# When half-finished weight sums are issued in a gated recurrence, and where its gate products stand: one change to a fused two-layer decoder kernel

## The chip, the cores and the metric

The kernel runs on one core of a Trainium2 chip. TensorE (PE) multiplies, VectorE (DVE) and ScalarE (ACT) do elementwise work, GpSimd (POOL) does small elementwise work and issues one queue of DMAs, SyncE (SP) issues the other queue. The metric is the device time of one execution in microseconds (us). The kernel before takes 2057.65 us, the median of three runs (2055.35, 2057.65, 2061.02).

## The reference, cut to what matters

Two layers on 1024 tokens of width 1024, all in float32. Layer 0 mixes tokens with a gated linear recurrence (HGRN2), layer 1 with a convolution module. Each mixer is followed by a residual layer norm, a squared-ReLU MLP of width 4096, and another residual layer norm.

```
proj = h @ w_in;  q, fz, v, g = split(proj, 4)              # layer 0
q = silu(q);  f = lb + (1 - lb) * sigmoid(fz);  k = 1 - f
S_t = diag(f_t) S_{t-1} + k_t v_t^T;   o_t = S_t^T q_t       # 8 heads of 128
o = o * rsqrt(mean(o^2) + 1e-6) * norm_g                     # a norm for each head
mix = (o * silu(g)) @ w_out                                  # the gate product
x = layer_norm(alpha * x + mix)
ff = square(relu(x @ ffn_w1[i])) @ ffn_w2[i]                 # up, then down
x = layer_norm(alpha * x + ff)
```

## The kernel before, in words

**Products.** A float32 product is made of three fp32r matmuls with a high and a low part of each operand (hi·hi, hi·lo, lo·hi). Most large products go by a fast 2x2 scheme: seven products of half-size blocks, of which several are of sums of blocks. Each of these seven is called a form; a raw weight block or a sum of blocks is cast to its high part by ACT, and DVE subtracts to get the low part. A form of the projections or of the up product is 12 or 24 matmuls of 128x512.

**Weight sums in DRAM.** The down product (`ffn_w2`) of each layer needs four sums of blocks for each of its eight slices of the inner width (chunks). They are made ahead, in DRAM, by DMAs that add on arrival. One set belongs to one chunk and has four sums. It starts with two plain copies of 1 MB (`L419`, `L420`), goes on with one adding DMA of 1 MB (`L421`), and then with two adding DMAs of 0.5 MB (`L423` twice), where each of these three needs the landing of what went before. Adding DMAs are issued from POOL. There are 16 sets, for two layers of eight chunks; the list `to_sum` gives their order. `block_sums` issues 12 of them in the recurrence stage, all from POOL. `sum_pieces` makes two more in the first MLP, after its chunks 0 and 2: seven pieces, one behind each form that follows, where the four copies (0.5 MB each, `L435`) go out from SP behind a tiny DMA that waits for the form (`L434`), and the three adds from POOL (`L440`). The last two sets are made later, in layer 1.

**The recurrence stage.** After the value projection, a loop runs over 12 pairs of column blocks (`PAIRS`: a pair makes the query and forget columns of one head, or the gate columns of two heads), 7 forms each. A form is cut into four slots of three matmuls, and each slot calls `slot()`, which is a tick. Python lists order everything: `later(n, job)` puts a job n ticks on, `step()` lets one or two heads' generators (`recurrence(h)`) go on by one of 18 steps, and two heads overlap, nine steps apart. So each engine's instruction order is written out by hand here; what waits at run time is decided by semaphores.

The steps that matter here: step 13 transposes the keys; step 14 makes the outer products for the state of four chunks of 128 tokens (`outer`), and one tick later DVE makes the chain of states (`chain`: a copy, then one instruction for each chunk); step 15 makes the outputs (`attend`), and one tick later comes the second chain and `settle(0)`; step 16 makes the other outputs, and one tick later comes `settle(1)`. A `settle` is the norm of half of the tokens for one head: ACT squares with a sum (`L755`), POOL a `tensor_scalar` (`L756`) and a power (`L538`), and four ticks later ACT scales the outputs (`L761`). Then PE transposes them (`give`), ACT takes them out (`L774`), and SP stores them in DRAM.

**The gate product.** `gate_turn`, called at every tick, loads a stored half-head (`u`) back, and when the gate for it is ready and nine ticks have gone by since that load, DVE multiplies them (`t<-u,t`, 128x512) and SP stores the result (`zd`). The last two heads do this in the seam, a list of jobs that runs beside the last pair and loads the output projection's weights.

**Order of the sums before.** In the pair loop, every sixth form starts a set: the first copy at once, the second 6 ticks on, the adds 12, 24 and 36 ticks on. POOL's order, with the norms between, follows from these ticks.

**The first MLP.** Up product: eight chunks of seven forms (the first two chunks have two of theirs made earlier). Weights are loaded and turned into forms three ahead (`fw.ahead(3)`). Beside this, `spare` turns weights of layer 1 into high and low parts and stores them (`ready`): DVE copies one column, POOL copies it on (`L1464`, `L1472`) so that the next load waits for it, ACT casts (`L1465`). From here on the order is not by hand: a scheduler with its own model of time sets it.

Of the kernel before, what the change touches and what calls it, by code (L numbers as in the profile page):

```python
# [8 lines left out]
F32 = mybir.dt.float32  # L9
# [3 lines left out]
ALU = mybir.AluOpType  # L13
PSUM = bass.MemoryType.PSUM

P = 128
# [3 lines left out]
H = 8  # L20
# [248 lines left out]
def body(ctx, tc, d, out):  # L269
    nc = tc.nc  # L270
# [128 lines left out]
    def block_sums(name, layer, c, after=None, gap=0, adds=None):  # L399
# [24 lines left out]
        for i, part in enumerate(parts):  # L424
            later((i + 1) * gap, part)

    def sum_pieces(name, layer, c):

        t = sums[name, layer, c] = dram.tile([4, P, 1024], F32, name=f"sum_{name}{layer}{c}")
        v, w = t.rearrange("a p n -> p a n"), d[name][layer, c].rearrange("a p n -> p a n")  # L430

        def copy(i, q):
            def go(after):
                nc.sync.dma_start(out=t[i : i + 1, 0, 0:1], in_=after)  # L434
                nc.sync.dma_start(out=v[:, i], in_=w[:, q])  # L435

            return go

        def add(out, x, **kw):
            return lambda after: nc.gpsimd.dma_start(out=out, in_=x, accum_op=ALU.add, **kw)  # L440

        def chained(i):
            return add(v[:, i], v[:, i - 1], max_dma_last_dim=4096)

        return [copy(0, 0), copy(1, 2), add(v[:, 0:2], w[:, 2:4]), copy(2, 0), chained(2), copy(3, 1), chained(3)]
# [208 lines left out]
    def recurrence(h):  # L654
# [159 lines left out]
        later(1, lambda: (chain(range(NTB, nk)), settle(0)))  # L814
        yield
        attend(range(NTB, 2 * NTB))
        later(1, lambda: settle(1))
        if h < H - 2:
            for half in range(2):
                load_values(2 * h + 2 + half)  # L820
# [110 lines left out]
    def gate_turn():  # L931
        now = ticks[0]
        if to_load and len(loaded) < 2 and done.get(to_load[0], now) <= now - 7:
# [1 line left out]
            u = p1("u")  # L935
            nc.sync.dma_start(out=u, in_=od[at[0]][at[1]])
            loaded.append((at, u, now))
        if loaded and loaded[0][0] in gates and loaded[0][2] <= now - 9:
            (h, half), u, _ = loaded.pop(0)
            g = gates.pop((h, half))  # L940
            mul(g, u, g)

            def store():
                nc.sync.dma_start(out=zd[half][:, h, :], in_=g)
                stored[h, half] = ticks[0]

            later(2, store)
# [79 lines left out]
    for p, (kind, j) in enumerate(PAIRS):  # L1027
# [7 lines left out]
        for i in ORDER:  # L1035
# [3 lines left out]
                    step()  # L1039
            pair_product(p, i, made.pop(0), st)  # L1040
            later(2, make_form)
            if (7 * p + ORDER.index(i)) % 6 == 1 and len(to_sum) > 4:
                block_sums(*to_sum.pop(0), gap=12)
        if kind == "q":
            later(4, lambda j=j: recs.append(j))
    early_out = ((0, 0), (1, 0), (2, 0))
# [9 lines left out]
    tick(100)  # L1056
    assert not waiting and not loaded and not to_load and not gates, (waiting, gates)
    order.close()
    oT = [o[0] for o in oT]


# [429 lines left out]
    for c in range(NFC):  # L1491
        for i in ORDER[2 if c < 2 else 0 :]:
# [4 lines left out]
            up.form(c, i, f)  # L1497
            if summing:
                summing.pop(0)(f[:1, 1, :1].bitcast(F32))
        if c in (0, 2):  # L1500
            summing += sum_pieces(*to_sum.pop(0))
        if c == 0:
            up.settle(1)
# [479 lines left out]
```

## Time and profile before

| what | value |
|---|---|
| median of three runs | 2057.65 us (2055.35 to 2061.02) |
| the profiled execution's own time | 2057.38 us |
| span of its trace | 2055.6 us |
| PE busy | 2024.2 us (98%) |
| mean granted TensorE clock | 0.998 |
| recurrence and seam in the trace | about 84 to 424 us |
| first MLP, chunks 1 to 7 | about 553 to 810 us |

How to read it: PE is busy nearly all the time, so the time can fall only where PE waits or where its clock is lower. An instruction's row in the timeline gives its start, its length, and in brackets the idle time of its engine just before, with what ended it. A row of the waits gives the total, the number of waits and the longest. A row of the windows gives the busy time of each engine in a stretch, the granted clock (1.00 is full) and the share of the 16 DMA engines that was busy; that share counts overlapping packets and reaches 1.08.

### The profile page before, as it was taken

The numbers are of one execution on the slowest core, as the hardware profiler recorded it, in microseconds if no ns is written. First come the engines' busy times: TensorE is split into PE (matmuls) and PEld (weight loads), VectorE is DVE, ScalarE is ACT, GpSimd is POOL, SyncE is SP. The second block draws the span as 40 slices with busy tenths as digits, with TensorE's granted clock in tenths as the row PEclk, the third lists the DMA queues.
The fourth block names the chain that finished last, engine by engine and source line by source line (L and its number), as shares of the span: only waits on it lengthen the run. The fifth ranks groups of instructions, "written<-read, shape, count | busy, mean of one in ns | idle before, by whom it ended". The sixth has DMA issues, their size and how long they took to land. (4 is left out here: it accounts for less than half of the span.)

```text
span 2055.6 us, 29682 instructions
## 1 busy us (share of the span) xinstructions
PE 2024.2 (98%) x11144; PEld 1669.3 (81%) x11144; DVE 1488.7 (72%) x1978; ACT 1092.3 (53%) x1725; POOL 394.7 (19%) x405
## 2 busy tenths in 40 slices
PE   8999999999999999999999999999999999999998
PEld 7888887888788888888888888888888888888886
DVE  8698887877866665666557898889589666754456
ACT  5456565631654655444443776488615555443343
POOL 0112232111000000000001799079210000100002
PEclk9999999999999999999999999999999999999999
DMA  4788999942399786999998755487659778995542
GB/s 187 216 206 229 263 244 250 268 185 89 125 324 298 275 302 215 374 341 325 336 339 294 303 185 187 191 329 268 255 210 344 247 236 299 392 293 195 194 154 103
DMA packets 183120, 517.55 MB, mean 252 GB/s; under 512 B 17984, under 2 KB 49856, under 8 KB 181824
## 3 DMA queue, kind: packets, MB, share of 16 engines
q1 hardware_dynamic: 167488, 456.93, 61.7%
q0 software_dynamic: 15488, 58.72, 12.3%
q8 instruction: 87, 1.43, 0.3%
q14 instruction: 57, 0.47, 0.1%
HBM read 380.85 MB, written 201.85 MB: 283 GB/s over the span
## 5 line engine op out<-in xcount | busy, mean ns | idle before, releaser
L204 PE MATMUL ps<-dw,dh 128*128 128x512 f32 x2688 | 611.6, 389 | 0.9 <-ACT dh L72 0.7
L204 PEld LDWEIGHTS ps<-dw,dh 128*128 128x128 f32 x2688 | 504.1, 188 | 106.3 <-ACT dh L72 1.1
L204 PE MATMUL ps<-x1f,fw 128*128 128x512 f32 x1344 | 307.8, 390 | 4.3 <-ACT fw L72 2.9
L204 PEld LDWEIGHTS ps<-x1f,fw 128*128 128x128 f32 x1344 | 251.4, 188 | 59.2 <-issue 2.7
L204 PE MATMUL ps<-xf,fs 128*128 128x512 f32 x1008 | 250.0, 399 | 3.5 <-issue 1.9
L204 POOL TENSOR_TENSOR cb<-cb,prod 128x512 f32<-128x512 f32 x168 | 222.5, 1333 | 14.4 <-ACT prod L1614 4.1
L204 PEld LDWEIGHTS ps<-xf,fs 128*128 128x128 f32 x1008 | 184.8, 189 | 42.8 <-issue 2.1
L204 DVE TENSOR_TENSOR dh<-dh 128x1024 fp32r<-128x1024 f32 x112 | 136.3, 1222 | 109.6 <-ACT dh L72 106.5
L204 DVE SCALAR_TENSOR_TENSOR ps<-u,par,ps 128x512 f32<-128x512 f32 x296 | 205.9, 749 | 10.7 <-ACT ps L1626 9.3
L204 PE MATMUL ps<-xa,wa 128*128 128x512 f32 x864 | 203.6, 393 | 1.3 <-DVE xa L204 0.9
L72 ACT CAST dh<-dh 128x1024 fp32r<-128x1024 f32 x112 | 117.2, 1050 | 146.3 <-DMA dh<-hf 141.2
L204 DVE TENSOR_TENSOR dw<-dr,dw 128x1024 fp32r<-128x1024 f32 x112 | 136.2, 1222 | 76.2 <-ACT dw L72 75.5
L204 PEld LDWEIGHTS ps<-xa,wa 128*128 128x128 f32 x864 | 160.2, 188 | 35.1 <-DVE xa L204 1.3
L72 ACT CAST dw<-dr 128x1024 fp32r<-128x1024 f32 x112 | 117.1, 1052 | 134.7 <-PE ps L204 114.0
L1614 ACT ACTIVATE prod<-u,par 128x512 f32<-128x512 f32 x168 | 119.2, 725 | 35.4 <-POOL cb L204 34.8
L538 POOL TENSOR_TENSOR mv<-mv,nhalf 128x1 f32<-128x1 f32 x32 | 42.2, 1319 | 403.9 <-DVE mv L204 393.6
L204 PE MATMUL ps<-w,oT 128*128 128x512 f32 x384 | 89.9, 392 | 1.3 <-ACT oT L952 0.8
L204 PE MATMUL ps<-xb,wa 128*128 128x512 f32 x384 | 91.1, 393 | 0.0
L204 PE MATMUL ps<-vw,xf 128*128 128x512 f32 x336 | 79.4, 398 | 6.1 <-ACT vw L455 5.5
L204 PEld LDWEIGHTS ps<-w,oT 128*128 128x128 f32 x384 | 71.4, 188 | 16.6 <-ACT oT L952 1.2
L204 PEld LDWEIGHTS ps<-xb,wa 128*128 128x128 f32 x384 | 71.1, 188 | 14.4
L1465 ACT CAST spare<-next 128x1024 fp32r<-128x1024 f32 x38 | 39.9, 1051 | 78.0 <-DMA next<-in_wpw_dram 23.9
(252 smaller groups left out, 2915.3 us busy)
## 6 DMA issues: line engine op xcount, KB each, us to landing
wa<-ready SPq DMA_DIRECT2D x140, 512.0 KB, 4.4
dh<-hf SPq DMA_DIRECT2D x112, 512.0 KB, 4.7
sum_w<-in_w_dram POOLq DMA_DIRECT2D x40, 1024.0 KB, 10.8
ready<-spare SPq DMA_DIRECT2D x76, 512.0 KB, 5.0
raw<-in_w1q_dram SPq DMA_DIRECT2D x66, 512.0 KB, 4.6
dr<-sum_w SPq DMA_DIRECT2D x64, 512.0 KB, 7.4
hf<-ht SPq DMA_DIRECT2D x112, 256.0 KB, 6.1
dr<-in_w_dram SPq DMA_DIRECT2D x48, 512.0 KB, 6.9
```

What stands on the lines that cost most here:

```text
L72: self.nc.scalar.copy(out=slot[:, 0, c], in_=raw[:, c])
L204: return op(*args, **kw)
L538: nc.gpsimd.tensor_tensor(out=dst, in0=src, in1=nhalf[:, :n], op=ALU.pow)
L1465: nc.scalar.copy(out=slot[:, 0].bitcast(F32R), in_=raw)
L1614: nc.scalar.activation(tp, u[:, k : k + HT], AF.Copy, scale=tap(j, k))
```

## The change

Three things change.

1. **Sums.** A new function, `sum_step`, replaces `block_sums` in the pair loop. Each call issues the next part of every set that is under way, and starts a new set if told so (two copies at once). It is called behind the forms 1, 3 and 5 of the first pair and the first form of the second pair, and from then on once for each head, in the job that holds `settle(1)`, right behind that norm's POOL instructions; for the last head twice. So a set takes four calls. Ten sets start in the recurrence stage instead of twelve.
2. **Gate products.** While a head stands between step 13 and step 15, a gate product needs 18 ticks since its load instead of nine.
3. **First MLP.** Sets in pieces follow chunks 0, 2, 3 and 4 instead of 0 and 2.

```diff
+    running = []
+
+    def sum_step(new):
+        for parts in list(running):
+            parts.pop(0)()
+            if not parts:
+                running.remove(parts)
+        if not new:
+            return
+        name, layer, c = of = to_sum.pop(0)
+        t = sums[of] = dram.tile([4, P, 1024], F32, name=f"sum_{name}{layer}{c}")
+        v, w = t.rearrange("a p n -> p a n"), d[name][layer, c].rearrange("a p n -> p a n")
+        nc.gpsimd.dma_start(out=v[:, 0:2], in_=w[:, 0:4:2])
+        nc.gpsimd.dma_start(out=v[:, 2:4], in_=w[:, 0:2])
+
+        def chained(i):
+            return lambda: nc.gpsimd.dma_start(out=v[:, i], in_=v[:, i - 1], accum_op=ALU.add, max_dma_last_dim=4096)
+
+        running.append([lambda: nc.gpsimd.dma_start(out=v[:, 0:2], in_=w[:, 2:4], accum_op=ALU.add), chained(2), chained(3)])
...
-        later(1, lambda: settle(1))
+        later(1, lambda: (settle(1), sum_step(len(to_sum) > 6), h == H - 1 and sum_step(False)))
...
-        if loaded and loaded[0][0] in gates and loaded[0][2] <= now - 9:
+        busy = any(13 <= one[2] <= 14 for one in active)
+        if loaded and loaded[0][0] in gates and loaded[0][2] <= now - (18 if busy else 9):
...
-            if (7 * p + ORDER.index(i)) % 6 == 1 and len(to_sum) > 4:
-                block_sums(*to_sum.pop(0), gap=12)
+            if p == 0 and ORDER.index(i) in (1, 3, 5) or (p, i) == (1, ORDER[0]):
+                sum_step(True)
...
-        if c in (0, 2):
+        if c in (0, 2, 3, 4):
             summing += sum_pieces(*to_sum.pop(0))
```

PE's order does not change anywhere. These are the places where the others' order does.

POOL around the two norms of the sixth head (h = 5), before. `sum_w` is a set's tile in DRAM, `ss` holds a norm's sums; a DMA that waits for a `DMASW` semaphore waits for the landing of an earlier DMA from POOL, and `L756` waits for ACT's squares:

```order
L423 DMA sum_w_2921<-sum_w_2921 128x1024 [waits DMASW0_49]
L421 DMA sum_w_3242<-in_w_dram 128x2x1024 [waits DMASW1_49]
L756 TENSOR_SCALAR ss<-ss 128x4 [waits Activation_49]
L538 TENSOR_TENSOR ss<-ss,nhalf 128x4 [waits Pool_49]
L756 TENSOR_SCALAR ss<-ss 128x4 [waits Activation_49]
L538 TENSOR_TENSOR ss<-ss,nhalf 128x4 [waits Pool_49]
L423 DMA sum_w_3242<-sum_w_3242 128x1024 [waits DMASW4_49,DMASW2_49]
```

The same place in the change (the norm's lines are now `L776` and `L558`):

```order
L445 DMA sum_w_2565<-in_w_dram 128x2x1024 [waits DMASW0_49]
L439 DMA sum_w_3066<-in_w_dram 128x2x1024 [waits DMASW5_49]
L440 DMA sum_w_3066<-in_w_dram 128x2x1024
L776 TENSOR_SCALAR ss<-ss 128x4 [waits Activation_49]
L558 TENSOR_TENSOR ss<-ss,nhalf 128x4 [waits Pool_49]
L776 TENSOR_SCALAR ss<-ss 128x4 [waits Activation_49]
L558 TENSOR_TENSOR ss<-ss,nhalf 128x4 [waits Pool_49]
L443 DMA sum_w_2241<-sum_w_2241 128x1024 [waits DMASW3_49]
L443 DMA sum_w_2565<-sum_w_2565 128x1024 [waits DMASW4_49,DMASW1_49]
```

The three DMAs ahead of the norms now belong to the call behind the head before, and the landings that they wait for were issued one head earlier still.

DVE at the third head's state chain (h = 2), before. `t<-u,t` is a gate product, `state` the chain, `fs` the low part of a form, `T` and `qk` belong to the head that overlaps:

```order
L204 TENSOR_TENSOR fs<-pr,fs 128x512
L204 TENSOR_TENSOR t<-u,t 128x512
L204 SCALAR_TENSOR_TENSOR t<-ps,sq 128x512
L204 TENSOR_TENSOR t<-u,t 128x512
L204 COPY state<-ps 128x128
L204 SCALAR_TENSOR_TENSOR state<-state,dec,ps 128x128 x3
```

The same place in the change:

```order
L204 TENSOR_TENSOR fs<-pr,fs 128x512
L204 SCALAR_TENSOR_TENSOR t<-ps,sq 128x512
L204 COPY state<-ps 128x128
L204 SCALAR_TENSOR_TENSOR state<-state,dec,ps 128x128 x3
L204 TENSOR_TENSOR kd<-qk,rt 128x2x128x4
L204 TENSOR_TENSOR qk<-qk,f 128x2x128x4
L204 TENSOR_TENSOR fs<-pr,fs 128x512
L204 SCALAR_TENSOR_TENSOR state<-state,dec,ps 128x128 x3
L204 TENSOR_TENSOR T<-f 128x128
L204 TENSOR_TENSOR T<-T 128x64
L204 TENSOR_TENSOR t<-u,t 128x512
L204 TENSOR_TENSOR t<-t,ps 128x512
```

Both products move behind the second chain. The same happens to one product each at two later heads.

POOL in the first MLP, behind the second set in pieces, before and then in the change. `spare` and `next` are the small copies that hold ACT's cast and the next load of layer 1's weights:

```order
L440 DMA sum_w_5890<-sum_w_5890 128x1024 [waits DMAHW5_49,DMAHW1_49,DMASW0_49]
L1464 COPY spare<-ss 128x1 [waits DMAHW6_49,DVE_49,Pool_49]
L1472 COPY next<-ss 128x1 [waits DMAHW0_49,DVE_49]
L1464 COPY spare<-ss 128x1 [waits DMAHW3_49,DVE_49,Pool_49]
L1472 COPY next<-ss 128x1 [waits DMAHW6_49,DVE_49]
```

```order
L460 DMA sum_w_5878<-sum_w_5878 128x1024 [waits DMAHW2_49,DMAHW5_49,DMASW7_49,DMASW6_49]
L1486 COPY spare<-ss 128x1 [waits DMAHW6_49,DVE_49,Pool_49]
L1494 COPY next<-ss 128x1 [waits DMAHW1_49,DVE_49]
L460 DMA sum_w_6163<-in_w_dram 128x2x1024 [waits DMAHW5_49,DMAHW7_49,DMAHW3_49,DMAHW2_49]
L1486 COPY spare<-ss 128x1 [waits DMAHW7_49,DVE_49,Pool_49]
L1494 COPY next<-ss 128x1 [waits DMAHW1_49,DVE_49]
L460 DMA sum_w_6163<-sum_w_6163 128x1024 [waits DMAHW0_49,DMAHW5_49,DMASW1_49,DMASW0_49]
```

Six more adding DMAs, each of which waits for landings, now stand between these small copies in the chunks that follow.

1 line of the change is left out of this document (added).

## The prediction

> **What bounds the kernel now.** The page comes first. PE is busy for all but 31 us of the span, so a change of order pays only where PE waits, or runs at less than its clock.
>
> ```profile
> span 2055.6 us, 29682 instructions
> PE 2024.2 (98%) x11144; PEld 1669.3 (81%) x11144; DVE 1488.7 (72%) x1978; ACT 1092.3 (53%) x1725; POOL 394.7 (19%) x405
> ```
>
> Next, the waits of PE in the recurrence stage and its seam (84 to 424 us), in us in total, times, longest. They add up to 9.1 us: no gain there can be larger, but for the clock.
>
> ```profile
> PE ps L204 <- ACT o L761: 2.4, 3, 1.1
> PE ps L204 <- issue: 1.9, 1, 1.9
> PE ps L204 <- DVE state L204: 1.4, 2, 0.9
> PE ps L204 <- ACT t L857: 0.9, 1, 0.9
> PE ps L204 <- ACT oT L952: 0.8, 1, 0.8
> PE ps L204 <- DVE t L204: 0.7, 2, 0.4
> PE ps L204 <- DVE oT L204: 0.5, 1, 0.5
> PE ps L204 <- ACT kt L744: 0.5, 1, 0.5
> ```
>
> The first two rows lead to POOL. Here is its timeline before the sixth head's first norm: `L421` sits 6.18 us on a landing, and the norm's `L756`, queued behind it, starts only when that DMA has been issued. Under it stand ACT, which then waits 3.15 us for the norm, and that kind of wait in total for the stage.
>
> ```profile
> 335.07 0.88 POOL L423 DMA_DIRECT2D sum_w<-sum_w  x1 [6.57 <-DMA sum_w<-sum_w]
> 342.12 1.20 POOL L421 DMA_DIRECT2D sum_w<-in_w_dram  x1 [6.18 <-issue]
> 343.40 0.92 POOL L756 TENSOR_SCALAR ss<-ss 128x4 f32<-128x4 f32 x1
> ...
> 345.46 1.14 ACT L761 ACTIVATE o<-ps,ss 128x128 f32<-128x128 f32 x4 [3.15 <-POOL ss L538]
> ...
> ACT o L761 <- POOL ss L538: 11.5, 8, 3.2
> ```
>
> PE's timeline shows what reaches it: two waits for `o`, and at 345 us a wait that the trace only calls issue.
>
> ```profile
> 268.52 0.66 PE L204 MATMUL ps<-ident,o 128*128 128x128 f32 x4 [1.06 <-ACT o L761]
> ...
> 347.28 1.49 PE L204 MATMUL ps<-xf,fs 128*128 128x512 f32 x4 [1.89 <-issue]
> ...
> 385.09 0.66 PE L204 MATMUL ps<-ident,o 128*128 128x128 f32 x4 [0.94 <-ACT o L761]
> ```
>
> Behind that longest wait the granted clock drops (the column behind POOL's):
>
> ```profile
> 346.00:348.00 2.00, 0.72 (x3) 0.63 (x3) 0.00 (x0) 2.00 (x13) 0.20 (x2) 0.94 1.08 243
> 348.00:350.00 2.00, 2.00 (x8) 1.60 (x8) 1.34 (x4) 1.59 (x6) 1.00 (x1) 0.50 1.08 223
> 350.00:352.00 2.00, 2.00 (x8) 1.59 (x7) 1.07 (x3) 1.97 (x5) 0.00 (x0) 0.71 1.03 265
> ```
>
> **Part 1, the sums behind the second norm.** Each adding DMA now finds its predecessors landed, because they were issued a head earlier (some 33 us; the longest wait on a landing above is 6.57 us), and no DMA that waits stands between a head's two norms. POOL then starts `L756` when ACT's squares end. What goes away: 1.06 + 0.94 = 2.0 us of waits for `o`. I also take the 1.89 us wait: without it PE would have met the same late ACT a form later, and it stands where the DMA share is 1.08, which the sums make. With it goes the clock loss: 2 x (0.06 + 0.50 + 0.29) = 1.7 us. Together 5.6 us. The bounds are 2.0 us, if the issue wait has nothing to do with the sums, and, with all other waits of the eight rows but those of the next part, 9.1 - 1.4 + 1.7 = 9.4 us.
>
> The clock gate deserves a check. The Trainium skill, TensorE: Matmul & The Clock Gate, section "What's actually happening", lets the gate fall to half only after a whole idle window of about 3.4 us. By it a wait of 1.89 us would not suffice, the 1.7 us would stay, and the forecast would be that much higher; the half-clock stretch here came right behind the wait, so I go by the rows.
>
> POOL's own work grows by nothing: five issues for each head, 0.9 to 1.2 us each, where POOL next has work a head later. The four sets at the start meet no norm. The bursts share the DMA engines with SP's loads, but the stage carries two sets fewer, and these two rows of the page give their price (MB, share of 16 engines over the span):
>
> ```profile
> q1 hardware_dynamic: 167488, 456.93, 61.7%
> q0 software_dynamic: 15488, 58.72, 12.3%
> ```
>
> That is 0.617 x 2055.6 / 456.93 = 2.78 us of all engines for a MB from SP, and 0.123 x 2055.6 / 58.72 = 4.31 us for one from POOL. Two sets of 4.2 MB take 36 us of engine time out of a stage of 340 us. I count no gain for it.
>
> **The seam pays.** Behind the seventh head's norms POOL now issues three adds (1.05 + 0.52 + 0.52 = 2.1 MB, 9.0 us of all engines), where `L423` went out alone (2.3 us), and behind the last head three more. SP's loads for the seam go out just then, and the engines are full there:
>
> ```profile
> 387.39 0.88 POOL L423 DMA_DIRECT2D sum_w<-sum_w  x1
> ...
> 396.00:400.00 4.00, 3.97 (x58) 3.05 (x52) 2.81 (x4) 3.74 (x8) 0.00 (x0) 1.00 1.02 394
> 400.00:404.00 4.00, 4.00 (x23) 3.12 (x21) 3.21 (x6) 3.94 (x7) 0.00 (x0) 1.00 1.07 401
> ```
>
> A shared queue delays those loads by up to 9.0 - 2.3 = 6.7 us. They were issued some ten ticks ahead, so most of it is covered: bounds 0 and 6.7, I take 1 us, near the low end, since no wait for a DMA is among PE's rows there.
>
> **Part 2, the gate products.** Two of them stand ahead of the third head's state chain, and PE waits 0.94 us for it; one ahead of the sixth head's, where PE waits 0.51 us.
>
> ```profile
> 217.08 0.68 DVE L204 TENSOR_TENSOR t<-u,t 128x512 f32<-128x512 f32 x1
> ...
> 218.28 0.68 DVE L204 TENSOR_TENSOR t<-u,t 128x512 f32<-128x512 f32 x1
> 218.88 0.28 DVE L204 COPY state<-ps 128x128 f32<-128x128 f32 x1
> ...
> 219.22 0.49 PE L204 MATMUL ps<-state,qk 128*128 128x128 f32 x2 [0.94 <-DVE state L204]
> ...
> 335.47 0.49 PE L204 MATMUL ps<-state,qk 128*128 128x128 f32 x2 [0.51 <-DVE state L204]
> ```
>
> Starts are 0.60 us apart, so two products held back bring the chain 1.2 us forward and one 0.6: both waits go, 1.4 us. Behind the chain the same products delay a form's low part by 1.2 us; forms are made two ahead, which covers it. If the cover is gone, up to 1.2 us come back. I take 1.4; bounds 0.2 and 1.4.
>
> **Part 3, two more sets in the first MLP.** One set in pieces is 2.1 MB from SP and 2.1 MB from POOL: 2.1 x 2.78 + 2.1 x 4.31 = 14.9 us of all engines. They fall on chunks 4 and 5, about 657 to 695 and 695 to 733 us; these are the windows of chunks 3 to 6:
>
> ```profile
> 618.00:657.00 39.00, 39.00 (x174) 32.30 (x173) 24.26 (x30) 18.72 (x28) 2.94 (x7) 1.00 0.90 288
> 657.00:695.00 38.00, 37.80 (x167) 30.68 (x166) 25.29 (x31) 22.55 (x33) 2.80 (x7) 1.00 0.97 327
> 695.00:733.00 38.00, 37.15 (x164) 30.46 (x163) 24.61 (x30) 22.41 (x33) 2.25 (x5) 1.00 0.72 250
> 733.00:771.00 38.00, 38.00 (x170) 31.45 (x169) 28.33 (x33) 22.94 (x34) 2.01 (x4) 1.00 0.83 296
> ```
>
> Chunk 4 has 0.97 x 38 = 36.9 us of engine work and gets 51.8; chunk 5 has 27.4 and gets 42.3. Over 38 us each that leaves 13.8 + 4.3 = 18.1 us behind, which chunks 6 and 7 take up. Forms are loaded three ahead, and one takes 24 matmuls of 307.8 / 1344 = 0.229 us (the first row below), so 16.5 us cover it, nearly all. Bounds: 0, because chunk 3 carried a set with PE busy throughout; and 18.1 less a cover of 9.6 (16.5 without a landing of 4.6, a cast of 1.05 and a subtraction of 1.22), 8.5 us. I take 2, nearer to chunk 3's row.
>
> ```profile
> L204 PE MATMUL ps<-x1f,fw 128*128 128x512 f32 x1344 | 307.8, 390 | 4.3 <-ACT fw L72 2.9 <-DVE c L204 1.1 <-ACT c L1286 0.2
> L1465 ACT CAST spare<-next 128x1024 fp32r<-128x1024 f32 x38 | 39.9, 1051 | 78.0 <-DMA next<-in_wpw_dram 23.9
> L204 DVE TENSOR_TENSOR dw<-dr,dw 128x1024 fp32r<-128x1024 f32 x112 | 136.2, 1222 | 76.2 <-ACT dw L72 75.5
> ...
> raw<-in_w1q_dram SPq DMA_DIRECT2D x66, 512.0 KB, 4.6
> ```
>
> **The sum.** -5.6 - 1.4 + 1 + 2 = -4.0 us. The profiled execution took 2057.38 us, 1.8 beyond its span and 0.3 under the median of 2057.65. So 2053.4 there and 2053.6 for the median: I say 2053.5 us.
>
> **The rivals.** *All of it is hidden*: no cost in the seam and the MLP, and the other waits of the stage (0.9, 0.7 and 0.5 us) go too, because ACT and DVE get on earlier. -5.6 - 1.4 - 1.5 = -8.5, about 2049 us. For it: chunk 3 hid its set without any wait. Against: those waits name DVE and ACT, not POOL.
>
> *The relief stops short*: the issue wait and its clock loss come from something else and stay, while the costs are as above: -2.0 - 1.4 + 3 = -0.4, about 2057 us. For it: no semaphore is named there. Against: of seven heads only one met it, and there ACT was held up longest.
>
> *The first MLP fills up* (the slower one). POOL's order is strict, so an add that waits for its copies holds up the small copies behind it, and ACT with them; chunk 4 shows this already:
>
> ```profile
> ACT spare L1465 <- POOL spare L1464: 9.6, 2, 8.9
> ```
>
> That wait of 8.9 us uses up the cover of 9.6. If a further set adds its own wait of this kind in chunks 4 and 5, the whole 18.1 us come through: -7.0 + 1 + 18.1 = +12.1, about 2069.5 us. It decides from a cost of 7.0 us on, where the gain is gone. Against it: behind that wait PE lost at most 0.85 us. The Trainium skill, DMA: Bandwidth & Descriptors, section "Issuing engines are not separate DMA queues", speaks on this side: whichever engine issues, all transfers share the same 16 engines, so moving sets does not make them cheaper. The 1.02 to 1.08 of the windows agree.
>
> **How the numbers follow.** Forecast 0.43 (its own range 2050.5 to 2057), all hidden 0.20, relief short 0.23, MLP full 0.14. A measurement of this kernel can tell 0.3%, 6.2 us, from no change: faster is under 2051.5, slower over 2063.8. Faster: 0.20 and 0.07 of the forecast's low end, 0.27. Slower: 0.14, and 0.01 for the rest, 0.15. The same: 0.58. The range of 8 in 10 takes in most of the hidden case and stops short of a full MLP: 2048.5 to 2063 us.
>
> **What would show it.** Right: `L761` has no wait over about 1 us for POOL, the waits of PE for `o` and `state` between 84 and 424 us are gone, and the clock is 1.00 throughout that stretch. Wrong: waits for landings in PE's or ACT's rows between 395 and 415 us (seam), waits of PE over 2 us in chunks 4 to 6 with a DMA share above 1.0 (MLP), or a wait called issue of 1 us or more elsewhere in the recurrence (relief short).

## The result: slower, and the profile after

The change is slower. Its median is 2070.51 us (six runs, 2067.77 to 2076.72) against 2057.06 us for the kernel before on the same chip; the ratio of the two is 1.0062, with a 95% interval of 1.0049 to 1.0076. The forecast was 2053.5 us with a range of 2048.5 to 2063.

The profiled execution of the change took 2076.72 us, the longest of its six, so a second trace of the same kernel was taken in another set of runs (2070.76 us). The order of PE's matmuls is the same in both kernels up to the end of the first MLP, so the trace can be cut at the same matmul. In this table each stage runs from the start of one matmul to the start of another (us), the first one from the start of the span. Stage A is the first 1293 matmuls of the recurrence (three heads begin in it), B the next 2057, C the 158 up to the first matmul of the output projection (the seam), D output projection and norm, E the first MLP's up product, F the rest.

| stage | before | change | change, second trace |
|---|---|---|---|
| value projection | 85.4 | 85.8 | 85.2 |
| A, start of the recurrence | 120.7 | 124.3 | 124.1 |
| B, most of the recurrence | 188.9 | 185.5 | 183.8 |
| C, seam | 19.2 | 28.5 | 26.5 |
| D, output projection, norm | 97.4 | 97.4 | 97.4 |
| E, first MLP, up product | 312.2 | 320.3 | 319.6 |
| F, the rest | 1223.6 | 1225.1 | 1224.3 |

Only B became shorter, and that is the stage the sums were moved for. A, C and E became longer by 3.4 to 3.6, 7.3 to 9.3 and 7.4 to 8.1 us.

These are the waits of PE in the recurrence and its seam after the change (total, times, longest), with ACT's wait for POOL's norms under them:

```profile
PE ps L204 <- DMA f<-vd: 5.7, 1, 5.7
PE ps L204 <- ACT t L877: 4.1, 3, 2.7
PE ps L204 <- DVE t L204: 3.0, 3, 1.8
PE ps L204 <- DVE blocks L204: 1.1, 1, 1.1
...
PE ps L204 <- ACT o L781: 0.4, 1, 0.4
...
ACT o L781 <- POOL ss L558: 2.5, 4, 1.0
```

ACT's wait for the norms fell from 11.5 to 2.5 us, and PE's waits for `o` from 2.4 to 0.4. The waits for `state` and the one called issue are gone. In their place stand waits that were shorter before or not there, the longest for a DMA.

That one is in the seam. Two loads, `f<-vd`, bring the last head's values, one for each half of the tokens. PE goes on 0.13 us after the first of them has landed (the landings named here are read from the semaphore records of the trace). In SP's queue (a row's length is the time that the issues took, with what they waited for between them) this load went out at 398.46 us, after a wait of 3.1 us for the landing of an earlier store of a gate product, `zd<-t`; the last line below is that wait. The store had taken 10.3 us to land, and the load then took 12.7. Ahead of all this POOL had issued its three adds (386.81 and 394.04). SP's next pair of loads, `back<-zd` (half-finished outputs), held the queue for 5.97 us:

```profile
386.81 1.83 POOL L443 DMA_DIRECT2D sum_w<-sum_w  x2
394.04 1.17 POOL L445 DMA_DIRECT2D sum_w<-in_w_dram  x1 [5.40 <-issue]
...
388.19 0.85 SPq L965 DMA_DIRECT2D zd<-t  x1
...
398.46 0.53 SPq L672 DMA_DIRECT2D f<-vd  x1
...
399.88 5.97 SPq L991 DMA_DIRECT2D back<-zd  x2
...
411.34 2.05 PE L204 MATMUL ps<-f,kt 128*128 128x128 f32 x8 [5.70 <-DMA f<-vd]
...
SPq L672 <- DMA zd<-t: 3.1, 1, 3.1
```

Before, that store took 4.9 us to land and the load 9.2, the load did not wait for a store, and the pair `back<-zd` took 1.27 us:

```profile
386.48 0.43 SPq L944 DMA_DIRECT2D zd<-t  x1
...
394.02 0.57 SPq L652 DMA_DIRECT2D f<-vd  x1
...
397.83 1.27 SPq L970 DMA_DIRECT2D back<-zd  x2
```

Behind the wait the clock was at half for some 6 us (the number before the last two of a window's row), and the DMA share stood above 1 for most of that time:

```profile
409.00:411.00 2.00, 0.00 (x0) 0.00 (x0) 0.50 (x1) 0.35 (x1) 0.00 (x0) 0.81 1.08 417
411.00:413.00 2.00, 1.66 (x8) 1.69 (x9) 0.00 (x0) 1.55 (x3) 0.00 (x0) 0.50 1.02 405
413.00:415.00 2.00, 2.00 (x7) 1.61 (x7) 1.47 (x5) 0.00 (x0) 0.00 (x0) 0.50 1.13 363
415.00:417.00 2.00, 2.00 (x9) 1.81 (x8) 1.01 (x1) 1.01 (x1) 0.00 (x0) 0.50 0.57 206
```

In the second trace the wait for `f` is 5.4 us, and the clock is low for a shorter time: 0.67 and 0.50 in the windows from 407 to 411 us, 0.97 in the next. That is most of the 2.0 us by which its stage C is shorter.

The gate products show a second new wait. ACT's copy of a projection into a tile `t` waits for the store of an earlier gate product, and PE waits for ACT:

```profile
235.39 0.58 ACT L877 COPY t<-ps 128x512 f32<-128x512 f32 x1 [3.67 <-DMA zd<-t]
...
236.03 4.62 PE L204 MATMUL ps<-xf,fs 128*128 128x512 f32 x12 [2.69 <-ACT t L877]
```

There are four tiles `t`. A product stands in one of them until its store has landed, so a product that is held back gives its tile back later.

### The profile page after: what moved, and what is told of

Same layout as the page of the kernel before. It is cut to its first block, busy times and chain, and to the rows that moved or that the text cites. A ratio compares the mean times of both kernels' runs of the same rounds, so it can differ in the third digit from the quotient of the medians.

```text
span 2074.9 us, 29700 instructions
## 1 busy us (share of the span) xinstructions
PE 2029.6 (98%) x11144; PEld 1673.0 (81%) x11144; DVE 1488.1 (72%) x1978; ACT 1092.3 (53%) x1725; POOL 390.5 (19%) x401
## 4 chain that ended last, share of the span: by engine, by line
PE 73%; DMA 10%; DVE 9%; ACT 3%; issue 3%; POOL 2%; SPq 0%; DVEq 0%; POOLq 0%; ACTq 0%
PE ps L204 73%; DMA hf<-hr 1%; POOL cb L204 1%; DMA y<-kept 1%; DMA dh<-hf 1%; DMA ready<-spare 1%; DMA dr<-in_w_dram 1%; DVE qk L204 1%; DMA raw<-in_w1q_dram 1%; DMA hf<-ht 1%; DMA zd<-t 1%; DVE t L204 1%; DMA vr<-in_wv_dram 1%; DVE y L204 1%; DMA f<-vd 1%
## 5 line engine op out<-in xcount | busy, mean ns | idle before, releaser
L204 PE MATMUL ps<-x1f,fw 128*128 128x512 f32 x1344 | 310.3, 392 | 9.8 <-DVE c L204 4.6
L558 POOL TENSOR_TENSOR mv<-mv,nhalf 128x1 f32<-128x1 f32 x32 | 42.2, 1320 | 390.5 <-DVE mv L204 380.2
L204 PEld LDWEIGHTS ps<-vw,xf 128*128 128x128 f32 x336 | 64.6, 193 | 21.0 <-ACT vw L475 5.0
```

Source lines behind the costliest of these rows:

```text
L204: return op(*args, **kw)
L558: nc.gpsimd.tensor_tensor(out=dst, in0=src, in1=nhalf[:, :n], op=ALU.pow)
```

## The experiments

All runs in one view: the ratio to the kernel before on the same chip with its 95% interval, and the stages of the table above in the run's one trace (us).

| kernel | ratio | A | B | C | D | E |
|---|---|---|---|---|---|---|
| before | 1 | 120.7 | 188.9 | 19.2 | 97.4 | 312.2 |
| the change | 1.0062 (1.0049 to 1.0076) | 124.3 | 185.5 | 28.5 | 97.4 | 320.3 |
| e8, the change again | 1.0063 (1.0040 to 1.0086) | 124.1 | 183.8 | 26.5 | 97.4 | 319.6 |
| e1, hold-back alone | 1.0010 (0.9996 to 1.0025) | 120.7 | 194.9 | 20.7 | 97.4 | 310.3 |
| e2, pieces alone | 1.0003 (0.9989 to 1.0016) | 120.7 | 185.4 | 19.9 | 97.4 | 316.9 |
| e3, change without hold-back | 1.0037 (1.0023 to 1.0051) | 124.4 | 182.8 | 27.1 | 97.4 | 314.8 |
| e4, change, seam's adds later | 0.9999 (0.9986 to 1.0011) | 124.1 | 183.8 | 19.2 | 97.5 | 313.5 |
| e5, hold-back, five tiles | 1.0028 (1.0018 to 1.0038) | 120.7 | 191.8 | 20.8 | 97.4 | 315.1 |
| e6, starts spread by forms | 1.0007 (0.9993 to 1.0021) | 124.2 | 182.8 | 19.2 | 97.4 | 316.7 |
| e7, e6 with two sets moved to the norm stage | 1.0083 (1.0061 to 1.0105) | 124.0 | 182.8 | 19.2 | 97.4 | 311.8 |
| e9, old order, two sets in the norm stage | 1.0021 (1.0010 to 1.0032) | 120.6 | 187.1 | 19.3 | 104.1 | 312.0 |
| e10, new order, three sets there | 1.0088 (1.0070 to 1.0106) | 120.7 | 183.1 | 19.3 | 117.7 | 317.2 |
| e11, seventh head's adds alone in the seam | 1.0037 (1.0022 to 1.0052) | 123.4 | 182.8 | 28.4 | 97.4 | 315.4 |
| e12, change, two sets moved to the norm stage | 1.0086 (1.0069 to 1.0104) | 123.8 | 185.5 | 28.4 | 104.8 | 317.7 |
| e13, change, two sets left out | 1.0047 (1.0034 to 1.0060) | 124.2 | 183.1 | 27.1 | 97.4 | 315.4 |
| e14, change, their adds left out | 1.0049 (1.0032 to 1.0065) | 122.5 | 185.2 | 28.3 | 97.4 | 320.6 |
| e15, new order, twelve sets | 0.9983 (0.9975 to 0.9992) | 120.6 | 185.1 | 19.3 | 97.4 | 311.1 |

Each stage is read from one execution. The two traces of the change itself differ by 1.7 us in B and 2.0 us in C, and stage F, which is not in the table, took 1221.6 to 1227.5 us over these traces. So a difference of under some 2 us in one stage is not told apart here.

### The parts one by one

**e1**, the hold-back alone, on the kernel before:

```diff
+        busy = any(13 <= one[2] <= 14 for one in active)
-        ... and loaded[0][2] <= now - 9:
+        ... and loaded[0][2] <= now - (18 if busy else 9):
```

> The kernel before with the hold-back of the gate products alone. Theory from the trace after: a product that is held back stores its result later, so its tile of the four t tiles comes free later, and ACT's copy of a projection into a t tile waits for that store (3.67 us for zd in the trace after, 2.69 us of PE behind it, and 1.6 us of lower clock): two waits for state go (1.4 us), one wait of some 2.7 us with its clock loss comes, about +3 us, 2060 us, with a wait of ACT's t copy for the landing of zd near 235 us. Rival: the store was only slow because of the new order of the sums; then the hold-back keeps its 1.4 us, 2055.7 us, and no such wait is there.

The wait that the theory named is there, and it was longer than expected. ACT's timeline and PE's in that run:

```profile
238.71 0.58 ACT L857 COPY t<-ps 128x512 f32<-128x512 f32 x1 [10.43 <-DMA zd<-t]
...
239.35 5.06 PE L204 MATMUL ps<-xf,fs 128*128 128x512 f32 x11 [9.46 <-ACT t L857]
```

PE stands still for 9.46 us, and stage B is 6.0 us longer. The ratio of 1.0010 is not clear of no change; the profiled execution was the longest of twelve, so the 6.0 us is a figure of that execution and not the typical cost. With the old order of the sums POOL's transfers went out at 225.5 and 226.1 us, just ahead of the store at 227.1; whether they delayed it was not tested.

**e5** gives the hold-back a fifth tile:

```diff
-    "t": (wide_t, 4), ... "state": ((P,), 8)
+    "t": (wide_t, 5), ... "state": ((P,), 4)
```

> The kernel before with the hold-back of the gate products and a fifth tile t (room for it comes from the ring of states, four instead of eight). Theory: the 9.5 us wait that the hold-back alone makes is a wait for a free tile t; with a fifth tile ACT's copy waits for no store, that wait goes, and what is left is the gain of the two waits for state, 1.4 us: ratio to the kernel before 0.9993, no wait of ACT over 1 us for zd near 230 us. Rival: the wait comes from the store itself being late in SP's queue and moves to the next product, so that a wait over 2 us for zd or t stays between 225 and 250 us and the ratio is 1.001 or more.

By what was on record the rival held: a wait of over 2 us stayed, and the ratio is 1.0028. One more tile let ACT's first copy through (227.78 us), but the next one waits for a store, and PE's wait fell from 9.46 to 4.98 us only:

```profile
237.83 0.59 ACT L857 COPY t<-ps 128x512 f32<-128x512 f32 x1 [6.38 <-DMA zd<-t]
...
238.47 5.49 PE L204 MATMUL ps<-xf,fs 128*128 128x512 f32 x12 [4.98 <-ACT t L857]
```

So tiles and late stores both have a part. The room came from the ring of `state`, four tiles instead of eight; no wait for `state` is among PE's rows in this run. How many tiles would be enough was not tried.

**e3** is the change without the hold-back:

```diff
-        ... and loaded[0][2] <= now - (18 if busy else 9):
+        ... and loaded[0][2] <= now - 9:
```

> The change without the hold-back of the gate products. Theory: the wait for zd at 232 to 236 us and its clock loss (4.3 us) go, the waits for state (1.4 us) come back: 2070.5 - 2.9 = 2067.6 us. Rival (the store is slow because of the sums alone): the wait stays, and the time with it, 2070 to 2072 us.

The wait for `zd` near 235 us is gone, and the two waits for `state` are back. Stage B is 182.8 us, 1.0 to 2.7 less than in the change, as the theory said. The median of 2066.3 us is a little lower than expected, and E was shorter too, which the theory did not say.

**e2**, pieces after four chunks and ten sets in the old order:

```diff
-            if (7 * p + ORDER.index(i)) % 6 == 1 and len(to_sum) > 4:
+            if (7 * p + ORDER.index(i)) % 6 == 1 and len(to_sum) > 6:
-        if c in (0, 2):
+        if c in (0, 2, 3, 4):
```

> The kernel before with sets in pieces after chunks 0, 2, 3 and 4 of the first MLP, and the sums of the recurrence in the old order, ten sets of them. Theory: the first MLP is full; between 545 and 860 us PE loses about 8 us more than before (waits for c and fw in chunks 2 to 5), less 0 to 2 us for the two sets that the recurrence is rid of: 2063 to 2066 us. Rival: the MLP's loss in the trace after belongs to that one long execution, and the MLP takes the two sets for 0 to 2 us: 2055 to 2060 us.

Neither as expected: E lost 4.7 us, not 8, and B won 3.5 us with nothing but two sets fewer. The two nearly cancel.

### The seam

**e4** moves the adds behind the seventh and eighth heads to the end of the recurrence:

```diff
-        later(1, lambda: (settle(1), sum_step(len(to_sum) > 6), h == H - 1 and sum_step(False)))
+        later(1, lambda: (settle(1), h < H - 2 and sum_step(len(to_sum) > 6)))
...
     tick(100)
+    for _ in range(3):
+        sum_step(False)
```

> The change, but the adds that it puts behind the norms of the seventh and eighth head are issued behind the last of the recurrence. Theory: the seventh head's three adds slow the landing of the gate product zd, SP's queue stands behind the loads that wait for it, and PE waits 5.7 us for the last head's values f; with the adds gone from there that wait falls under 1 us and the clock stays at 1.00: 2070.5 - 6 = 2064.5 us. Rival: SP's queue is late because of the order of its own transfers and of the hold-back of the gate products; then the wait of 5.7 us for f stays, and the time is 2069 to 2072 us.

The theory held, and more was won than it asked for: C is back at 19.2 us, no wait for `f` is left among PE's rows, and the ratio is 0.9999. That is 0.0063 under the change (some 13 us), of which C explains 7.3 to 9.3; another 6 to 7 us are in E, whose order shifted with the edit.

**e11** puts only the seventh head's three adds back (with no hold-back and the starts of e6):

```diff
+        later(1, lambda: (settle(1), h < H - 1 and sum_step(len(to_sum) > 6)))
```

> As the run with spread starts, but the three adds behind the seventh head's norm stand where the change has them; only those of the eighth head go out later. Theory: these three adds alone make the seam's loss: from the last wait for blocks near 393 us to the first product of the output projection 26.5 us instead of 19.2, with a wait of over 5 us for f; ratio 1.004. Rival: the eighth head's adds share in it, then the wait for f is under 3 us and the ratio under 1.0025.

C is 28.4 us, so these three alone make the loss. PE's wait changed its name: it is put down to ACT's copy of the keys, which stands in ACT's queue behind a cast that waited 2.84 us for a weight load and then waited for a store itself. The load `f<-vd` landed in the same moment (406.30 us, ACT's copy ended at 406.32, PE went on at 406.43), so PE had to wait for it as in the change:

```profile
PE ps L204 <- ACT kt L764: 6.0, 2, 5.6
...
401.98 1.04 ACT L972 CAST w<-raw 128x1024 fp32r<-128x1024 f32 x1 [2.84 <-DMA raw<-in_wout_dram]
405.84 0.48 ACT L764 COPY kt<-ps 128x384 f32<-128x384 f32 x1 [2.20 <-DMA od<-kt]
```

SP's `back<-zd` took 6.30 us here too. Several of the seam's transfers are late at once.

### The start

**e6** is the change without the hold-back, with e4's seam, and its first four sets started at other forms:

```diff
-            if p == 0 and ORDER.index(i) in (1, 3, 5) or (p, i) == (1, ORDER[0]):
+            if 7 * p + ORDER.index(i) in (1, 6, 11, 16):
```

> The change without the hold-back and with the seam's adds behind the recurrence, and its four first sets started behind the forms 1, 6, 11 and 16 of the recurrence instead of 1, 3, 5 and 7. Theory: the burst of four starts delays the loads of weights at 95 to 125 us and costs 3.5 us by 210 us; spread, it costs under 1 us, and the time is that of the change with the seam's adds later (ratio 0.9999) less 3 for the starts and less 3 for the hold-back: ratio 0.997. Rival: the loads are late because the engines are full there in any order (their share was 0.97 before), then waits of 1 to 2 us stay between 100 and 130 us and the ratio is 0.9985.

A stayed at 124.2 us, as the rival has it, and the ratio is 1.0007. The reason is in POOL's timeline. Ahead of the first norm nothing ties POOL to PE, so it issues as fast as its own DMAs land, whichever form a start stands behind: the copy of the second set (`L439`) goes out at 85.84 us in the change and at 85.54 in e6, in both while the first add is under way. What counts there is POOL's order. The change, then e6's copy, then PE's waits in the change up to 210 us:

```profile
80.69 1.22 POOL L445 DMA_DIRECT2D sum_w<-in_w_dram  x1 [5.03 <-DMA sum_w<-in_w_dram]
85.84 0.71 POOL L439 DMA_DIRECT2D sum_w<-in_w_dram  x1 [3.93 <-issue]
94.54 0.68 POOL L440 DMA_DIRECT2D sum_w<-in_w_dram  x1 [7.99 <-DMA sum_w<-in_w_dram]
...
85.54 0.71 POOL L439 DMA_DIRECT2D sum_w<-in_w_dram  x1 [3.60 <-issue]
...
PE ps L204 <- DVE t L204: 2.6, 2, 1.8
```

**e10** orders it otherwise, an add between the starts (and puts three sets into the norm stage, below):

```diff
+            if 7 * p + ORDER.index(i) in (1, 4, 7, 10, 13, 16):
+                sum_step((7 * p + ORDER.index(i)) % 6 == 1)
...
+        for _ in range(min(3, len(quiet))):
+            quiet.pop(0)(y[half][:1, t, :1])     # a piece behind a norm's rows
```

> Sums behind the second norms as in the change, without the hold-back, the seam's adds behind the recurrence; three starts instead of four ahead of the first norm, each a step after the adds of the one before (calls at the forms 1, 4, 7, 10, 13 and 16); three sets in pieces in the norm stage, two in the MLP as before. Theory: the 3.5 us that the change loses before 210 us come from POOL running ahead with too much at once, so with three starts it loses under 1.5 us there; from 210 to 393 us it keeps its gain of 6.1 us, the seam and the MLP lose nothing: ratio 0.997 to 0.998. Rival: the loss before 210 us stays at 3.5 us (the engines are full there in any order), ratio 0.9985 to 0.9995.

A is 120.7 us again: the next copy now stands behind an add that waits 11.92 us, and 1 MB less is in flight while the weights of 89 to 96 us are loaded.

```profile
80.06 1.22 POOL L445 DMA_DIRECT2D sum_w<-in_w_dram  x1 [4.99 <-DMA sum_w<-in_w_dram]
93.19 0.89 POOL L443 DMA_DIRECT2D sum_w<-sum_w  x1 [11.92 <-DMA sum_w<-in_w_dram]
93.76 1.05 POOL L439 DMA_DIRECT2D sum_w<-in_w_dram  x1
...
PE ps L204 <- DVE t L204: 0.7, 2, 0.4
```

There are also only three starts here instead of four. That does not matter for A: the change's fourth start goes out at 128.69 us, when the loss is already there (PE's last wait of this kind ends at 125.26).

B and C are as hoped too (183.1, 19.3). But D grew by 20.3 us, and the kernel as a whole is slow.

### Sets in the norm stage

Before the MLP the DMA share is low (0.28 between 434 and 545 us before), so sets were tried there, in pieces behind the norm of each 128 tokens: three in e10, two in **e9** (old order, ten sets) and two in **e12** (the change, with pieces after chunks 0 and 2 alone). The edit of e9 and e12:

```diff
+    made_of = [sum_pieces(*to_sum.pop(0)) for _ in range(2)]
+    quiet = [pieces[k] for k in range(7) for pieces in made_of]
...
         keep(half, t, y[half][:, t, :])
+        for _ in range(min(2, len(quiet))):
+            quiet.pop(0)(y[half][:1, t, :1])
```

> The kernel before with ten sets in the recurrence in the old order and two sets in pieces in the stage of the output projection and the first norm (each piece behind a norm's rows), the first MLP as before with pieces after chunks 0 and 2. Theory: two sets fewer in the recurrence are worth 2.9 us there (first form to output projection 326.0 us in the run with the old order and ten sets, against 328.9 before), and the quiet stage and the MLP lose under 1 us: ratio 0.9985 to 0.999. Rival: the adds hold up POOL's powers of the norms, PE's waits between the recurrence and the MLP grow by 2 us or more, and the ratio is 1.000 or above.

> The change, but the two sets that it puts into the first MLP after chunks 3 and 4 are made in pieces in the norm stage before it (pieces after chunks 0 and 2 as before). Theory: the MLP's loss of 7.4 to 8.0 us in both traces of the change comes from these two sets, and it falls to 0 to 3 us: ratio 1.0025 to 1.004. Rival: the MLP's loss is a matter of how its instructions happen to be ordered, not of the sets: it stays at 5 us or more, ratio 1.005 to 1.006.

The rival of e9 held: D grew by 6.7 us in e9 and 7.4 in e12. POOL's queue tells why. In e10 a norm's power (`L558`) stands behind three adds of which each waits, and PE waits 18.14 us for what follows from it:

```profile
463.79 1.20 POOL L460 DMA_DIRECT2D sum_w<-in_w_dram  x1 [7.09 <-DMA sum_w<-in_w_dram]
474.54 1.16 POOL L460 DMA_DIRECT2D sum_w<-in_w_dram  x1 [9.54 <-issue]
482.89 1.15 POOL L460 DMA_DIRECT2D sum_w<-in_w_dram  x1 [7.20 <-issue]
483.61 1.03 POOL L558 TENSOR_TENSOR mv<-mv,nhalf 128x1 f32<-128x1 f32 x1
...
486.61 1.97 PE L204 MATMUL ps<-ident,y 128*128 128x128 f32 x8 [18.14 <-DVE x1f L204]
```

It is the pattern that the change removed from the recurrence. In e12 E was 317.7 us, still 5.5 above before without the two sets in it, which by its wording is the rival's case. But it was no clean test of the MLP, since the stage before it ran late and may shift E as well.

**e7** puts two sets there on top of e6, with plain copies that nothing held back:

```diff
     assert not running and len(to_sum) == 6
+    sum_step(True)      # twice; each add goes behind the power of one norm
```

> As the run with spread starts, but two of the four sets in pieces leave the first MLP (pieces after chunks 0 and 2, as before) and are made between the recurrence and the MLP, where the DMA share was 0.28: copies behind the recurrence, each add behind the power of one norm. Theory: the two sets in the MLP cost 1.3 to 4.6 us and the quiet stage takes them for nothing: ratio 0.995 to 0.9965. Rival: the MLP takes the sets for nothing, and the ratio is that of the run with spread starts, within 0.001; or the adds hold up POOL's powers in the norms, and PE's waits between 440 and 545 us grow by over 1 us.

It does not answer its question: with no dependence to hold them, both sets went out at the very start of the program (POOL's first copy at 1.32 us, the last add at 53.46), and the value projection took 107.2 us instead of 85.4 (ratio 1.0083, 1.0061 to 1.0105). E, with pieces after chunks 0 and 2, was 311.8 us.

### The first MLP

**e8** repeats the change, and the wait for `f` came again (5.4 us), as did 319.6 us for E.

> The change itself once more, for a second trace of its first MLP. Theory: the wait of 5.7 us for f in the seam and the wait for zd near 235 us come again within 0.5 us, for they follow from orders; the MLP from its first form to its last again takes some 320 us, 8 more than before. Rival: the MLP's loss is an accident of that execution, and it takes 313 to 316 us here.

**e13** leaves the two further sets out, **e14** only their six adds:

```diff
-        if c in (0, 2, 3, 4):
+        if c in (0, 2):
             summing += sum_pieces(*to_sum.pop(0))
+        elif c in (3, 4):
+            sums[to_sum.pop(0)] = sums["w2", 1, 0]
```

```diff
+            pieces = sum_pieces(*to_sum.pop(0))
+            summing += pieces if c < 3 else [pieces[k] for k in (0, 1, 3, 5)]
```

> The change, with the two further sets of the first MLP left out (their slices of the down product take another slice's sums, so that no work stands in for them). Theory: the sets cost what the MLP loses: it takes 311 to 314 us from its first to its last form (320 in the change, 312.2 before), and the ratio falls to 1.0025 to 1.0035. Rival: it takes 317 us or more without them, so the loss comes from how the work before and around it is ordered, and the ratio stays at 1.005.

> The change, with the copies of the two further sets kept and their six adds left out (so those sums are unfinished). Theory: the adds hold up POOL's small copies, and ACT's cast and DVE with them, so that without the adds the MLP takes 314 us or less (320 in the change). Rival: the share of the DMA engines decides; the copies are 4.2 MB of the 8.4 MB and the MLP still takes 316 to 318 us.

Without the sets E is 315.4 us, in the middle between the two expectations: by these traces they cost 4.2 to 4.9 us of the change's 7.4 to 8.1, and about 3.2 us stay without them. Without their adds E is 320.6 us, so by its trace the copies from SP are enough to make the loss. The times of all runs do not confirm it: the ratio is 1.0049 without the adds and 1.0047 without the sets. e14's profiled execution was the longest of its six and e13's the shortest of its five, and in e14 a set's copies stand behind four forms in a row and not spread over seven. Which half of a set costs more stays open. These are PE's waits in the MLP of e14 and of e13 (`c` is a block of the up product on its way out, which ACT and DVE handle, `fw` a form):

```profile
PE ps L204 <- ACT c L1308: 4.1, 3, 2.4
PE ps L204 <- DVE c L204: 3.3, 3, 2.1
```

```profile
PE ps L204 <- ACT c L1308: 3.7, 3, 1.9
...
PE ps L204 <- DVE c L204: 0.6, 2, 0.4
```

PE waits for `c`, that is for ACT and DVE, and hardly for forms. What held DVE up can be read from the change's trace. The sum for a later form waits for a load of up weights, and the work on `c` stands behind that sum in DVE's order:

```profile
709.53 1.18 SPq L135 DMA_DIRECT2D raw<-in_w1q_dram  x1
...
719.05 1.22 DVE L204 TENSOR_TENSOR sum<-raw 128x1024 f32<-128x1024 f32 x1 [1.86 <-DMA raw<-in_w1q_dram]
...
723.33 4.84 PE L204 MATMUL ps<-x1f,fw 128*128 128x512 f32 x13 [1.92 <-DVE c L204]
```

That load took 9.4 us to land. PE's waits over 0.3 us for DVE's `c` all stand behind such a load: 4.3 and 3.4 us in the two traces of the change, 3.1 in e14, 0.4 in e13 and 0.9 before. What e13 keeps is a wait of 1.9 us for ACT's `c`, behind a cast of `spare` that waited 8.4 us for POOL's small copy, with a stretch of half clock after it; POOL had stood idle for 14.7 us ahead of that copy, for a landing of `hf<-hr` and not at an add.

Over all traces with 97.4 us for stage D, E took 310.3 to 315.4 us with two sets in pieces (before, e1, e5, e7, e13 and e15) and 313.5 to 320.3 with four (e4 is within 0.1 us in D). The two ranges overlap, so some 3 us either way come from how the work of ACT and DVE falls, and why it falls worse in the change than before stays open.

### What is left of the idea

**e15** keeps twelve sets in the recurrence, in the new order. Its edit is against the kernel before, so there is no hold-back, and pieces follow chunks 0 and 2; `sum_step` takes the number of starts here:

```diff
+        later(1, lambda: (settle(1), h < H - 2 and sum_step(2 if h < 3 else 1)))
+            if 7 * p + ORDER.index(i) in (1, 4, 7, 10, 13, 16):
+                sum_step((7 * p + ORDER.index(i)) % 6 == 1)
```

> Twelve sets in the recurrence as before, in the new order behind the second norms: three starts ahead of the first norm with steps between them, two starts behind each of the first three heads and one behind the next three; nothing behind the seventh and eighth; no hold-back, pieces after chunks 0 and 2. Theory: nothing is lost before 210 us, in the seam or in the MLP, and from 210 to 393 us most of the 6.1 us is kept, 4 to 6: ratio 0.997 to 0.998, faster than both kernels. Rival: the gain there came from the two sets fewer, not from the order; with twelve sets it is under 2 us, ratio 0.999 to 1.0005.

The ratio is 0.9983 (0.9975 to 0.9992): 2054.04 us against 2057.92, faster than both kernels, by a little less than expected. B is 185.1 us, 3.8 less than before, with as many sets, and 2.3 more than with ten sets in this order. A wait of 1.7 us for a tile `t` is part of that difference, without any hold-back (near 231 us); the DMA share between 200 and 360 us is 0.94 to 0.98, against 0.62 to 0.79 in the change. In its trace F is 1227.3 us, 3.7 longer than before, for a reason that was not looked for.

```profile
PE ps L204 <- ACT t L879: 2.5, 2, 1.7
PE ps L204 <- DVE state L204: 1.5, 2, 0.9
```

## Why the prediction was wrong

The forecast took 7.0 us off and put 3 us on. By the runs the sums took 6.1 us off, and the rest of the change put 19 to 24 on in its two traces. The gain was there; what failed are the covers that were to hide the costs, and one cost that was put at nothing.

**Part 1, the sums behind the second norm: right in size, in part by luck.** The prediction took 5.6 us out of the heads' stretch. Stage B without the hold-back is 182.8 us in e3, e6 and e11, 6.1 less than before; the waits for `o` fell to 0.4 us in total, and the issue wait and the half clock behind it are gone. What was wrong is where it came from. "Two sets fewer ... I count no gain for it": with the old order and ten sets B is shorter by 3.5 (e2) and 1.8 us (e9). With the new order and twelve it is shorter by 3.8 (e15). Order and number share the gain, and the order with twelve sets gave 3.8 us, not 5.6. The 1.7 us of clock in it is a matter of chance: e2 and e9 have the same order and number of sets, and in both PE waits 2.4 us for `o` near 267 us, yet the clock behind it stays at 1.00 in e2 and falls to 0.55 and 0.60 for two windows in e9.

**The starts: costed at nothing, 3.4 to 3.6 us.** "The four sets at the start meet no norm" is true, but they meet SP's loads of weights, and a bare POOL runs ahead of PE there. An add between the starts took that loss away (e10, e15). Over all traces with the change's starts, or with e6's, the loss is 1.8 to 3.7 us.

**The seam: +1 forecast, 7.3 to 9.3 measured, beyond the bound of 6.7.** The cause was named, the place too, but the step "they were issued some ten ticks ahead, so most of it is covered" failed. It took each load by itself. In SP's queue the load of the last head's values first waited 3.1 us for the landing of a store that took 10.3 us instead of 4.9, and then took 12.7 us to land itself instead of 9.2, so two delays of one cause added up. Then the stop of 5.7 us cost the clock on top, which no bound included.

**Part 2, the gate products: -1.4 forecast, +1.0 to +2.7 in the change and +6.0 alone, in one trace.** Over all six traces with the hold-back and the new order the cost is 0.3 to 2.7 us. Both waits for `state` went, as forecast. The failed step is "behind the chain the same products delay a form's low part ...; forms are made two ahead, which covers it". It followed DVE's queue and not the tile that the product occupies, nor its store. Who waits for the moved step was asked for the result, not for the space.

**Part 3, the MLP: +2 forecast, 7.4 to 8.1 measured, inside its bounds of 0 to 8.5.** The sets cost 4.2 to 4.9 of it by the trace of e13. The term was put too low, and the failed step is its cover, "16.5 without a landing of 4.6, a cast of 1.05 and a subtraction of 1.22". It counts forms in stock and a load that lands in 4.6 us. PE did not run out of forms. It waited for `c`, which stood in DVE's order behind the wait for a load that took 9.4 us.

**The rival that the time resembles.** The full MLP gave 2069.5 us, and 2070.5 was measured, but by another sum. Its mechanism, adds that hold up the small copies and ACT, is not borne out by the traces: without the adds E is as long (e14), and ahead of the small copy that ACT waited longest for in the change (8.1 us) POOL stood idle 14.4 us for DVE, not at an add. As said, the times of all runs do not part the two. Its point of decision, 7.0 us, was reached in the MLP only just; the slowdown needs the seam, the start and the gates as well. The differences of the first trace, stage by stage: +3.6 - 3.4 + 9.3 + 8.1 + 1.5 in F and 0.4 ahead of A = 19.5, against 19.34 between the two profiled times.

One sum among the rivals is off: "all hidden" takes 1.5 us for three waits that add up to 2.1, so its time would be 2048.6 us and not 2049. Nothing hangs on it.

The costs were set near the low end each for its own reason, but three of them, the start, the seam and the MLP, have one cause: more transfers at a place where the engines are full. So they came together. The Trainium skill, DMA: Bandwidth & Descriptors, section "Issuing engines are not separate DMA queues", says that transfers interleave on the same 16 engines whoever issues them; the seam bears it out, where three adds of POOL's made SP's `back<-zd` take 5.97 us instead of 1.27.

## What to carry to other kernels

When a transfer is moved, follow the queue of every engine that has transfers of its own at the new place: there a load that must wait for an earlier landing goes out late, and then lands late as well. When a computation is held back, count the time that its tile and its store stay occupied, not only the engine. And test each part alone: here one part was worth 6 us, and four others beside it took that back three to four times over.

## What the runs showed of the hardware

**The same wait sometimes costs clock and sometimes does not.** In the first MLP PE has a wait of 1.47 us for `fw` in nearly every trace. Of all traces only e1, e2 and e12 show a lower clock behind it. In e1 the granted clock is 0.50 and 0.66 for two windows, and 21 matmuls take 6.65 us; in e4 it stays at 1.00, and 18 take 4.77:

```profile
545.67 6.65 PE L204 MATMUL ps<-x1f,fw 128*128 128x512 f32 x21 [1.47 <-ACT fw L72]
...
546.00:548.00 2.00, 2.00 (x6) 1.56 (x5) 2.00 (x3) 1.23 (x2) 0.52 (x1) 0.50 0.65 168
548.00:550.00 2.00, 2.00 (x7) 1.56 (x7) 2.00 (x3) 0.00 (x0) 2.00 (x1) 0.66 0.27 102
```

```profile
535.40 4.77 PE L204 MATMUL ps<-x1f,fw 128*128 128x512 f32 x18 [1.47 <-ACT fw L72]
...
537.00:539.00 2.00, 1.93 (x9) 1.56 (x9) 2.00 (x3) 0.00 (x0) 1.78 (x1) 1.00 0.55 213
```

A wait of 2.48 us in e4 (near 234 us) cost no clock either. The slow stretch in e1 is seven matmuls that start 0.427 us apart instead of 0.228, some 1.4 us more. So a wait is priced at its length, or at its length and 1.4 us, and one trace does not tell which. The Trainium skill, TensorE: Matmul & The Clock Gate, section "What's actually happening", describes windows of about 3.4 us that run freely, which fits a price that depends on where the wait falls; that the gate needs a whole idle window does not fit, since 1.47 us were enough here.
